# ScalarE's evacuations of PSUM banks take TensorE's order in the attention; GpSimd's sums in the recurrent mixer's gates go to VectorE

## The chip, the cores and the metric

The program runs on one core of a Trainium2 chip. A core has five engines that take their instructions in order, each from its own queue: TensorE (PE in the profile; its weight loads are PEld), VectorE (DVE), ScalarE (ACT), GpSimd (POOL) and SyncE (SP), which here only starts transfers. Matmul results land in PSUM, which this kernel divides into eight banks of 128 x 512 float32. The metric is the device time of one execution in microseconds (us).

## The reference, cut to what matters

Two layers run over 1024 positions of width 1024. Layer 0 mixes tokens with dilated window attention, layer 1 with a gated linear recurrence (HGRN2). Behind each mixer stand an output projection, a layer norm, a squared-ReLU MLP and another layer norm.

```python
for i in range(DEPTH):                      # DEPTH = 2
    if i % 2 == 0: y = dilated_attention_mixer(x, attn_w_in, attn_w_out)
    else:          y = hgrn2_mixer(x, hgrn_w_in, hgrn_w_out, hgrn_norm_g, lbs[i])
    x = layer_norm(ALPHA * x + y, ...)
    x = layer_norm(ALPHA * x + square(relu(x @ w_up)) @ w_down, ...)

# attention: 16 heads of 64, three groups (window, dilation) = (128,1), (512,4), (2048,16):
#   rotary q and k, a banded softmax, p @ v, then a mix of the three groups
#   by their softmax denominators

# hgrn2_mixer, 8 heads of 128, chunks of 64 positions:
log_f = logaddexp(log(lb), log1p(-lb) + log_sigmoid(z))    # z = forget projection
key   = (1 - lb) * sigmoid(-z)
b     = cumsum(log_f)                                      # inside a chunk
q_dec, k_dec = silu(q_raw) * exp(b), key * exp(-b)
kv    = einsum(key * exp(b_last - b), v)                   # one 128 x 128 matrix a chunk
state = exp(b_last) * state + kv                           # scan over 16 chunks
o     = causal(q_dec @ k_dec.T) @ v + q_dec @ state
```

## The kernel before, in words

All large products are float32 split into a high and a low part, so each product is three matmuls: high by high, high by low and low by high. The attention's input projection and both MLPs also use a seven-product scheme for 2 x 2 blocks.

**Attention.** `attention` walks 252 steps n: 12 groups of two units (a unit is a pair of heads in one dilation group), in each group the seven block products `ORDA = (2, 1, 6, 7, 4, 5, 3)`, in each of these three columns j. A step calls `product(n)`: 12 matmuls (lines 820 to 822) into a bank of the kind `mm` (there are three), and then the bank is read into SBUF. For i = 2, 6, 7, 4 ScalarE copies it (lines 843, 847, 849, 851, to tiles `e`, `vp`, `vT`), for i = 1, 5, 3 VectorE adds it. The next step of that column, where it goes on in the same bank, has to wait for this copy. Behind the product the step runs pieces of the group before: scores (`s`, two banks), transposes of the probabilities (`ppt`, line 636) or of v (`vpt`), copied by ScalarE to `pts` (line 639) or `vn` (line 546), the product with v (lines 665 and 667) into the one bank of the kind `o`, copied by ScalarE to `og` (lines 627, 673 and 676), and the transposes of the softmax statistics (`mpt`, lines 711 and 714), which use the bank `o` too and so wait until `og` was copied out. `vpt`, `ppt` and the broadcasts `fb` share the two banks `pt`. Last the step prepares weights five steps ahead: ScalarE rounds them to the high part (`H`, line 487), VectorE subtracts for the low part (line 495).

**What sets the order.** `in_order` ties TensorE's and VectorE's instructions of these steps to the order in which they are written. ScalarE is not tied (but for steps 30 to 33): a scheduler that estimates durations puts its instructions into a queue order before the program runs, and on the chip the queue is then strictly in order. `behind(i, names)` adds an order between instructions of one engine without a semaphore.

**Recurrent mixer.** `hgrn` runs 8 heads. For each head, three projections (forget, query, input) by two halves, then `gate`: for the forget projection a chain of ScalarE passes (absolute value, exponential, logarithm) and VectorE passes over 128 x 1024 (head 0: twice 128 x 512) that ends in `ls` (the log of the forget gate), a scan `a` (line 1854), the sum `z + a1` on GpSimd (line 1856), and two exponentials; for the query projection another chain with a sum on GpSimd (line 1870). The pieces of a head run during the projections of the next head: `kv(0)` and `kv(1)` (line 1771) fill banks with the chunks' matrices, VectorE runs the recurrence over them (line 1780, states 1 to 7 in `stA`, 8 to 15 in `stB`), and `omat(0)`, `omat(1)` (lines 1793 and 1798) multiply by the states. `omat(1)` writes into a bank `s` that the recurrence of `kv(1)` must have read first.

## Time and profile before

| what | value |
|---|---|
| median of 3 runs | 2743.94 us (2741.07 to 2744.34) |
| the profiled execution's own time | 2744.21 us |
| its span, first to last instruction | 2742.4 us |
| mean granted TensorE clock | 0.997 |
| busy: PE, DVE, ACT, POOL | 98%, 75%, 51%, 3% |
| PE busy in 0 to 900 us (attention) | 882.08 of 900 |
| PE busy in 900 to 1045 us (its tail, the output projection) | 138.16 of 145 |
| PE busy in 1045 to 1680 us (MLP) | 630.61 of 635 |
| PE busy in 1680 to 2040 us (recurrent mixer) | 356.58 of 360 |
| PE busy in 2040 to 2742 us (output projection, MLP) | 693.77 of 702 |

Busy time is a union of intervals; idle time of PE in a stretch is the stretch less the busy time. A row of a timeline gives start and length in us, engine, line, operation, tiles, shape and count; the bracket behind it gives the idle time before it and what ended that. In the list of waits the three numbers are the total, the count and the longest wait.

### The profile page before, as it was taken

The page shows a single profiled execution, that of the slowest core. Times are in us where ns is not written, and L with a number is a line of the kernel's source. Part 1 is how long each engine was busy: PE and PEld are TensorE (multiplying, and loading weights), DVE is VectorE, ACT ScalarE, POOL GpSimd, SP SyncE. Part 2 cuts the span into 40 slices and gives each one's busy share as a digit, 9 for nine tenths or more (in the row PEclk, how much of TensorE's full clock was granted, in tenths as well). Part 3 has the DMA queues.
Part 4 walks back from the last instruction along what each step waited for, and adds up shares of the span by engine and source line. Part 5 has one row for each costly group of instructions (what it writes and reads, how often), then busy time and mean ns, then how long its engine had stood idle before and what let it go on. Part 6 is the DMA issues. An engine that isn't in the chain of part 4 may idle for free.

```text
span 2742.4 us, 44173 instructions
## 1 busy us (share of the span) xinstructions
PE 2701.2 (98%) x16256; PEld 2200.8 (80%) x16256; DVE 2055.6 (75%) x3876; ACT 1385.1 (51%) x3043; POOL 68.8 (3%) x46
## 2 busy tenths in 40 slices
PE   9999999999999999999999999999999999999998
PEld 7787887787787777888888888788878888888887
DVE  8868877787787778776696687566578886678687
ACT  5554555455554556444554345555552544445443
POOL 0000000000000002000000000011100100000000
PEclk9999999999999999999999999999999999999999
DMA  8877666767767434554575752011232464485653
GB/s 300 273 223 230 210 219 198 234 204 234 227 214 257 115 109 156 192 194 150 204 268 165 239 169 93 32 47 47 74 127 100 157 221 163 150 299 181 220 179 127
DMA packets 208153, 493.67 MB, mean 180 GB/s; under 512 B 30016, under 2 KB 44864, under 8 KB 207936
## 3 DMA queue, kind: packets, MB, share of 16 engines
q1 hardware_dynamic: 206688, 489.53, 53.1%
q8 instruction: 128, 2.10, 0.3%
q10 hardware_dynamic: 1248, 1.31, 0.2%
q14 instruction: 89, 0.73, 0.1%
HBM read 362.69 MB, written 94.11 MB: 167 GB/s over the span
## 4 chain that ended last, share of the span: by engine, by line
PE 87%; DVE 7%; ACT 2%; DMA 2%; issue 1%; SPq 0%; POOL 0%; DVEq 0%; ACTq 0%; POOLq 0%
PE pmm L822 7%; PE pmm L820 7%; PE pmm L821 7%; PE pup L1342 7%; PE pup L1340 7%; PE pup L1341 7%; PE pdy L1491 4%; PE pdy L1495 4%; PE pdy L1494 4%; PE pdx L1494 3%; PE pdx L1495 3%; PE pdx L1491 3%; PE pmm L192 3%; PE pmm L193 3%; PE pmm L194 3%; PE pmm L206 2%
## 5 line engine op out<-in xcount | busy, mean ns | idle before, releaser
L820 PE MATMUL pmm<-xh,H 128*128 128x512 f32 x1008 | 404.5, 401 | 1.5 <-ACT H L487 1.5
L822 PE MATMUL pmm<-xh,H 128*128 128x512 f32 x1008 | 396.2, 393 | 3.2 <-DVE H L495 2.9
L821 PE MATMUL pmm<-xl,H 128*128 128x512 f32 x1008 | 394.4, 391 | 0.8 <-DVE xl L158 0.7
L822 PEld LDWEIGHTS pmm<-xh,H 128*128 128x128 f32 x1008 | 189.8, 188 | 48.4 <-DVE H L495 7.7
L820 PEld LDWEIGHTS pmm<-xh,H 128*128 128x128 f32 x1008 | 190.5, 189 | 39.9 <-ACT H L487 2.6
L821 PEld LDWEIGHTS pmm<-xl,H 128*128 128x128 f32 x1008 | 190.5, 189 | 38.3 <-DVE xl L158 1.6
L1491 PE MATMUL pdy<-dT,dS 128*128 128x512 f32 x512 | 199.2, 389 | 0.0
L1494 PE MATMUL pdy<-dT,dS 128*128 128x512 f32 x512 | 199.2, 389 | 0.0
L1495 PE MATMUL pdy<-dT,dS 128*128 128x512 f32 x512 | 199.2, 389 | 0.0
L157 ACT ACTIVATE dS<-dr 128x512 fp32r<-128x512 f32 x192 | 119.3, 622 | 67.4 <-PE pdy L1495 36.4
L192 PE MATMUL pmm<-f0nh,wh 128*128 128x512 f32 x384 | 153.3, 399 | 0.0
L193 PE MATMUL pmm<-f0nl,wh 128*128 128x512 f32 x384 | 149.9, 390 | 0.0
L194 PE MATMUL pmm<-f0nh,wl 128*128 128x512 f32 x384 | 149.8, 390 | 0.0
L158 DVE TENSOR_TENSOR dS<-dr,dS 128x512 fp32r<-128x512 f32 x192 | 131.3, 684 | 8.9 <-ACT dS L157 8.9
L583 ACT ACTIVATE p<-p,stats 128x192 f32<-128x192 f32 (+1 forms) x256 | 108.7, 428 | 53.8 <-DVE stats L580 53.5
L157 ACT ACTIVATE dT<-hold 128x512 fp32r<-128x512 f32 x128 | 80.1, 626 | 80.6 <-DVE hold L1470 33.2
L1301 ACT ACTIVATE H<-wc 128x512 fp32r<-128x512 f32 x128 | 77.2, 625 | 78.5 <-DVE wc L1294 47.8
L1494 PEld LDWEIGHTS pdy<-dT,dS 128*128 128x128 f32 x512 | 96.1, 188 | 20.0
L1495 PEld LDWEIGHTS pdy<-dT,dS 128*128 128x128 f32 x512 | 96.1, 188 | 20.0
L1491 PEld LDWEIGHTS pdy<-dT,dS 128*128 128x128 f32 x512 | 96.1, 188 | 19.8
L580 DVE CUSTOM_DVE_ANT_0 p<-s,mask 128x192 f32<-128x192 f32 (+1 forms) x256 | 70.7, 332 | 45.0 <-PE s L567 32.3
L487 ACT ACTIVATE H<-wc 128x512 fp32r<-128x512 f32 x108 | 66.5, 629 | 70.1 <-DVE wc L479 67.5
(430 smaller groups left out, 6924.8 us busy)
## 6 DMA issues: line engine op xcount, KB each, us to landing
xh<-xtd SPq DMA_DIRECT2D x110, 512.0 KB
xl<-xtd SPq DMA_DIRECT2D x110, 512.0 KB
dr<-hd SPq DMA_DIRECT2D x192, 256.0 KB
dr<-in_w_down_dram SPq DMA_DIRECT2D x128, 256.0 KB
rot<-e SPq DMA_DIRECT2D x192, 128.0 KB
wa<-in_w_up_dram SPq DMA_DIRECT2D x48, 512.0 KB
wb<-in_w_attn_dram SPq DMA_DIRECT2D x36, 512.0 KB
wa<-in_w_attn_dram SPq DMA_DIRECT2D x33, 512.0 KB
```

Of the source, the lines that this page charges most:

```text
L157: act(hi, raw, AF.Copy)
L192: nc.tensor.matmul(o, wh[:, k], xs.h(k), start=k == 0, stop=False)
L193: nc.tensor.matmul(o, wh[:, k], xs.l(k), start=False, stop=False)
L194: nc.tensor.matmul(o, wl[:, k], xs.h(k), start=False, stop=k == NK - 1)
L820: nc.tensor.matmul(o, wh, hi[k // 2][:, c], start=begin and k == 0, stop=False, skip_group_check=True)
L821: nc.tensor.matmul(o, wh, lo[k // 2][:, c], start=False, stop=False, skip_group_check=True)
L822: nc.tensor.matmul(o, wl, hi[k // 2][:, c], start=False, stop=end and k == 3, skip_group_check=True)
L1340: nc.tensor.matmul(o, wh, xf.h(b, k), start=begin and k == 0, stop=False, skip_group_check=True)
L1341: nc.tensor.matmul(o, wh, xf.l(b, k), start=False, stop=False, skip_group_check=True)
L1491: nc.tensor.matmul(o[q], h, T_[:, L], start=begin, stop=False, skip_group_check=True)
L1494: nc.tensor.matmul(o[q], h, T_[:, R], start=False, stop=False, skip_group_check=True)
L1495: nc.tensor.matmul(o[q], l, T_[:, L], start=False, stop=end, skip_group_check=True)
```

## The change

**In the attention** a helper `evict` replaces `act` at every ScalarE copy out of a PSUM bank: the products' copies, `vn`, `pts`, `og`, `ml` and `sr`. It notes the instruction, and when the loop over the steps is done, each noted instruction is put `behind` the one noted before it. So these copies keep the order in which they are written, which is the order in which TensorE fills the banks. The other ScalarE instructions (`H`, the exponentials) are as free as before. The copies of the last group's pieces, which run after the loop, are not tied.

**In the gates** the constants change: `low` is exp(-max(C, -43)), C keeps only what lies below -43, `nA` is -A, `CA` is gone. The first logarithm takes `low` as scale and bias, so that it yields log(1 + E) less the bound's term C in one pass; with that the pass of VectorE on line 1852 (add C, then maximum with A) and the one on line 1853 (add) become one. Both sums of GpSimd are now VectorE's.

```diff
     def attention(pre, hc):
+        out_of = []
+        def evict(*args, **kw):
+            act(*args, **kw)
+            out_of.append(latest())
...
-                    act(vn[:, j * 512:(j + 1) * 512], pt, AF.Copy)
+                    evict(vn[:, j * 512:(j + 1) * 512], pt, AF.Copy)
...
         order.__exit__()
+        for i, j in zip(out_of, out_of[1:]):
+            behind(j, [i.name])
+        out_of.clear()
...
-        CA = c8("CA")
-        v.tensor_sub(CA, C, A)
+        low = c8("low")
+        v.tensor_scalar(low, C, -43.0, None, op0=ALU.max)
+        v.tensor_sub(C, C, low)
+        act(low, low, AF.Exp, scale=-1.0)
+        nA = c8("nA")
+        v.tensor_scalar(nA, A, -1.0, None, op0=ALU.mult)
...
                 act(a1, z, AF.Abs)
                 act(a1, a1, AF.Exp, scale=-1.0)
-                act(a1, a1, AF.Ln, bias=one)
+                act(a1, a1, AF.Ln, scale=low[:, hd:hd + 1], bias=low[:, hd:hd + 1])
                 nc.vector.scalar_tensor_tensor(ls, z, 0.0, a1, op0=ALU.min, op1=ALU.subtract)
                 nc.vector.scalar_tensor_tensor(z, z, 0.0, a1, op0=ALU.max, op1=ALU.add)
-                act(a1, ls, AF.Abs, bias=CA[:, hd:hd + 1])
+                act(a1, ls, AF.Abs, bias=nA[:, hd:hd + 1])
                 act(a1, a1, AF.Exp, scale=-1.0)
                 act(a1, a1, AF.Ln, bias=one)
-                nc.vector.tensor_scalar(ls, ls, C[:, hd:hd + 1], A[:, hd:hd + 1], op0=ALU.add, op1=ALU.max)
-                nc.vector.tensor_add(ls, ls, a1)
+                nc.vector.scalar_tensor_tensor(ls, ls, A[:, hd:hd + 1], a1, op0=ALU.max, op1=ALU.add)
                 nc.vector.tensor_tensor_scan(a1, sm[:, c], ls, 0.0, op0=ALU.mult, op1=ALU.add)
-                nc.gpsimd.tensor_add(z, z, a1)
+                nc.vector.tensor_add(z, z, a1)
...
-                nc.gpsimd.tensor_add(a3, a3, cur["a"][:, c])
+                nc.vector.tensor_add(a3, a3, cur["a"][:, c])
```

The diff moves instructions, and three places show how. A row gives the line, the operation, the tiles written and read, the shape and a count.

The first place is ScalarE's queue in the attention, in the third group, around the statistics `sr` that the profile has at 265.8 us. Of the kernel before:

```order
L849 ACTIVATE e<-pmm 128x512
L639 ACTIVATE pts<-ppt 128x384 x2
L487 ACTIVATE H<-wb 128x512
L849 ACTIVATE vp<-pmm 128x512
L851 ACTIVATE e<-pmm 128x512
L849 ACTIVATE e<-pmm 128x512
L676 ACTIVATE og<-o 128x2x256
L487 ACTIVATE H<-wc 128x512
L716 ACTIVATE sr<-mpt 32x128
```

And of the changed kernel, where L361 is the line in `evict` and L493 is the rounding of `H`:

```order
L361 ACTIVATE e<-pmm 128x512
L493 ACTIVATE H<-wb 128x512
L361 ACTIVATE e<-pmm 128x512
L361 ACTIVATE og<-o 128x2x256
L361 ACTIVATE pts<-ppt 128x384 x2
L493 ACTIVATE H<-wc 128x512
L361 ACTIVATE vp<-pmm 128x512
L493 ACTIVATE H<-wc 128x512 x2
L361 ACTIVATE e<-pmm 128x512
L361 ACTIVATE sr<-mpt 32x128
```

The second copy of `e` and the copy of `og` stood behind `pts`, `vp` and a copy of the next block product; now they stand ahead of all three. The order of TensorE's and VectorE's instructions in the attention is the same as before.

The second place is VectorE's queue in the recurrent mixer, in the second head (the profile has it from 1728 us), with the recurrence of the first head in between. Before:

```order
L1780 SCALAR_TENSOR_TENSOR stA<-stA,dec,kvps 128x128 x3
L1853 TENSOR_TENSOR ls<-ls,a_17045 128x1024
L1780 SCALAR_TENSOR_TENSOR stA<-stA,dec,kvps 128x128
L1854 SCALAR_TENSOR_TENSOR a_17045<-smask,ls 128x1024
L1780 SCALAR_TENSOR_TENSOR stA<-stA,dec,kvps 128x128 x2
L1780 SCALAR_TENSOR_TENSOR stB<-stA,dec,kvps 128x128
```

Now (L1793 is the recurrence, L1865 the joined pass, L1866 the scan, L1868 the sum that was GpSimd's):

```order
L1793 SCALAR_TENSOR_TENSOR stA<-stA,dec,kvps 128x128 x3
L1865 SCALAR_TENSOR_TENSOR ls<-ls,hc_A,a_17047 128x1024
L1793 SCALAR_TENSOR_TENSOR stA<-stA,dec,kvps 128x128
L1866 SCALAR_TENSOR_TENSOR a_17047<-smask,ls 128x1024
L1793 SCALAR_TENSOR_TENSOR stA<-stA,dec,kvps 128x128
L1868 TENSOR_TENSOR ze<-ze,a_17047 128x1024
L1793 SCALAR_TENSOR_TENSOR stA<-stA,dec,kvps 128x128
L1793 SCALAR_TENSOR_TENSOR stB<-stA,dec,kvps 128x128
```

State 7, the last one in `stA`, now comes behind the sum over 128 x 1024.

The third place is TensorE's queue at the same moment, the end of `omat(0)` of the first head. Before:

```order
L1793 MATMUL ho<-vn,aT 64x128 x2
L1798 MATMUL ho<-stA,qe 64x128 x2
L1771 MATMUL kvps<-vn,k2n 64x128 x14
L192 MATMUL pmm<-f0nh,wh 128x512
```

Now:

```order
L1806 MATMUL ho<-vn,aT 64x128 x2
L1811 MATMUL ho<-stA,qe 64x128
L1784 MATMUL kvps<-vn,k2n 64x128 x3
L1811 MATMUL ho<-stA,qe 64x128
L1784 MATMUL kvps<-vn,k2n 64x128 x11
L192 MATMUL pmm<-f0nh,wh 128x512
```

Three of the next matrices' matmuls moved ahead of the one that reads state 7. It is the only change in TensorE's order.

## The prediction

> **What bounds the kernel now.** I read the page's first part, then the list of TensorE's waits, then the timelines around the longest of them. The page:

> ```profile
> span 2742.4 us, 44173 instructions
> PE 2701.2 (98%) x16256; PEld 2200.8 (80%) x16256; DVE 2055.6 (75%) x3876; ACT 1385.1 (51%) x3043; POOL 68.8 (3%) x46
> ```

> TensorE is busy for 2701.2 of 2742.4 us. The change removes none of its matmuls, so it can win only out of the 41.2 us in which TensorE idles, and out of time in which its clock is low. The waits of TensorE (releaser; total, count, longest):

> ```profile
> PE mpt L714 <- ACT og L676: 6.4, 3, 2.1
> PE mpt L711 <- ACT og L673: 3.0, 3, 1.0
> PE pmm L822 <- DVE H L495: 2.9, 5, 1.2
> ...
> PE ho L1798 <- DVE stB L1780: 1.6, 1, 1.6
> ...
> PE ho L1793 <- DVE stB L1780: 1.4, 1, 1.4
> ```

> The two longest entries are one pattern: the transposes of the statistics need the bank `o`, which ScalarE has not copied out yet. The last two belong to the recurrent mixer. All other entries are start-up, weights or the layers' ends, which the change does not touch.

> **Attention: the six waits for `og`.** The first long one:

> ```profile
> 254.50 0.39 PE L822 MATMUL pmm<-xh,H 128*128 128x512 f32 x1
> 256.33 0.22 PE L667 MATMUL o<-pts,vn 64*64 64x64 f32 x1
> 260.14 0.60 ACT L849 ACTIVATE vp<-pmm 128x512 f32<-128x512 f32 x1 [1.68 <-PE pmm L822]
> 263.34 0.60 ACT L851 ACTIVATE e<-pmm 128x512 f32<-128x512 f32 x1 [2.60 <-PE pmm L822]
> 263.84 0.59 ACT L849 ACTIVATE e<-pmm 128x512 f32<-128x512 f32 x1
> 264.31 1.08 ACT L676 ACTIVATE og<-o 128x512 f32<-128x512 f32 x1
> 265.45 0.33 PE L714 MATMUL mpt<-ident,stats 128*128 128x128 f32 x1 [2.14 <-ACT og L676]
> ```

> The product for the second `e` ends by 254.9, the bank `o` is full at 256.55. ScalarE could copy both then, but its queue has `vp` and the next product's `e` (L851) ahead, and these wait for TensorE (1.68 and 2.60 us of idleness). So `og` starts 7.8 us after its data and TensorE stands for 2.14 us. In the changed queue both stand ahead of `pts` and `vp`. ScalarE then does `e` (0.59), `og` (1.08) and two `pts` from about 256.6 and is done by 259.2; `vp` is ready at 260.1, and TensorE comes to `mpt` at 263.3. The wait is gone with 4 us to spare. The 1.0 us kind is the same, one dilation group on:

> ```profile
> 414.18 0.19 ACT L583 ACTIVATION_READ_ACCUMULATOR p<-p,stats 128x1 f32 x1
> ...
> 417.56 0.60 ACT L851 ACTIVATE e<-pmm 128x512 f32<-128x512 f32 x1 [2.13 <-PE pmm L822]
> ...
> 418.52 0.61 ACT L673 ACTIVATE og<-o 128x512 f32<-128x512 f32 x1
> ```

> Here four exponentials now come ahead of `e`, `og` and `pts`. At this place of the profile the last of them ends at 414.4, so `og` (0.61) behind one `e` (0.60) is out by about 415.6, against about 418.1 where TensorE wants the bank (1.0 us before `og` ends). Two `pts` get late by some 3 us, to about 416.5; the next transposes, which need their banks, start here:

> ```profile
> 417.36 0.82 PE L636 MATMUL ppt<-ident,p 128*128 128x128 f32 x6
> ```

> That leaves about 0.9 us, the thinnest cover of the change; without it the 1.0 us would be back. I take off 6.4 + 3.0 = **9.4 us**. The order among the copies costs nothing by itself: none is put behind one that TensorE fills later, so no copy waits longer than its own data needs. SP's queue now has one weight load behind the four small loads of `ml` and one copy of `vT`:

> ```profile
> 271.78 0.54 SPq L460 DMA_DIRECT2D wa<-in_w_attn_dram  x1
> ...
> 283.84 1.67 ACT L487 ACTIVATE H<-wa 128x512 fp32r<-128x512 f32 x3
> ```

> It is issued 12 us ahead of its rounding, so a shift by five such issues costs 0.

> **The clock behind these waits.** A table of stretches (length, PE, PEld, DVE, ACT, POOL, granted clock, DMA share, GB/s) and one matmul:

> ```profile
> 263.00:273.00 10.00, 7.86 (x70) 6.17 (x72) 4.93 (x7) 5.01 (x9) 0.00 (x0) 1.00 0.98 358
> 494.00:504.00 10.00, 8.35 (x44) 6.62 (x46) 4.13 (x7) 4.56 (x9) 0.00 (x0) 0.83 0.85 324
> 726.00:736.00 10.00, 8.01 (x36) 6.28 (x38) 4.48 (x7) 4.90 (x9) 0.00 (x0) 0.83 0.90 337
> 1046.00:1054.00 8.00, 5.76 (x17) 3.94 (x17) 6.35 (x12) 2.06 (x5) 0.52 (x1) 0.79 0.50 183
> ...
> 498.52 0.63 PE L820 MATMUL pmm<-xh,H 128*128 128x512 f32 x1
> ```

> Behind two of the three waits of 2.1 us the clock falls, and a matmul takes 0.63 instead of 0.39 us. The loss is 10 x (1 - 0.83) = 1.7 us each time. Where the wait is gone I expect the dip gone: 2 x 1.7 = **3.4 us**. The dip at 1046 follows other waits (8 x 0.21 = 1.7 us); it stays in my sum, and may go or stay with the changed phase.

> [...]

> **Gates: VectorE and GpSimd.** The second head, in order of time:

> ```profile
> 1732.17 2.28 DVE L1854 TENSOR_TENSOR_SCAN a<-smask,ls 128x1024 f32<-128x1024 f32 x1
> 1734.38 0.70 DVE L1780 SCALAR_TENSOR_TENSOR stA<-stA,dec,kvps 128x128 f32<-128x128 f32 x2
> 1741.95 1.22 DVE L1869 SCALAR_TENSOR_TENSOR a<-qe,a 128x1024 f32<-128x1024 f32 x1
> 1743.24 2.35 POOL L1870 TENSOR_TENSOR a<-a,a 128x1024 f32<-128x1024 f32 x1 [6.29 <-DVE rms L1808]
> 1743.41 2.20 DVE L1809 TENSOR_SCALAR rms<-rms 128x4 f32<-128x4 f32 x1
> 1745.53 1.21 DVE L158 TENSOR_TENSOR wl<-wr,wh 128x1024 fp32r<-128x1024 f32 x1
> 1746.74 0.34 DVE L1780 SCALAR_TENSOR_TENSOR stB<-stB,dec,kvps 128x128 f32<-128x128 f32 x1
> ...
> 1743.64 0.44 PE L1793 MATMUL ho<-vn,aT 128*64 128x128 f32 x4 [1.39 <-DVE stB L1780]
> 1747.13 0.43 PE L1798 MATMUL ho<-stB,qe 128*64 128x128 f32 x2 [1.55 <-DVE stB L1780]
> ```

> A VectorE operation on 128 x 4 takes 2.20 us, because it lies under GpSimd's sum (2.35 us) and ends with it; the rounding (1.21) comes next, and only then the last state. TensorE waits 1.39 + 1.55 = 2.94 us. The bare sums on VectorE take what a like pass takes, 1.22 us. Per head VectorE loses the 2.2 us under GpSimd once or twice and the pass of line 1852, and gains two passes:

> ```profile
> L1856 POOL TENSOR_TENSOR ze<-ze,a 128x1024 f32<-128x1024 f32 (+1 forms) x9 | 19.3, 2148 | 296.3 <-ACT a L1866 108.6 <-DVE a L1854 85.7 <-DVE rms L1808 67.6
> L1852 DVE TENSOR_SCALAR ls<-ls,hc_C,hc_A 128x1024 f32<-128x1024 f32 x7 | 5.7, 808 | 1.3 <-ACT a L1849 1.3
> ```

> That is -0.81 + 2 x 1.22 = +1.63 us of work against up to 4.4 us unblocked. In the changed queue states 14 and 15 stand ahead of the pass of line 1869, so from about 1741.7 nothing of `omat(1)` waits: **-2.94 us**.

> But a new wait appears at state 7. The scan ends at 1734.45; state 6 takes 0.26, the moved sum 1.14, state 7 0.26: 1736.1. TensorE without it:

> ```profile
> 1734.75 0.82 PE L1798 MATMUL ho<-stA,qe 128*64 128x128 f32 x4 [0.19 <-DVE stA L1780]
> 1735.49 1.09 PE L1771 MATMUL kvps<-vn,k2n 64*64 64x128 f32 x28
> ```

> It would begin state 7's matmul at 1735.1, and the three matmuls moved ahead fill 0.2 us. I take **+0.8 us** (bounds 0, if the queue slips as it did before, and 1.1).

> In the later heads TensorE does not wait before, though only just:

> ```profile
> 1783.37 0.34 DVE L1780 SCALAR_TENSOR_TENSOR stB<-stB,dec,kvps 128x128 f32<-128x128 f32 x1
> 1783.65 0.44 PE L1793 MATMUL ho<-vn,aT 128*64 128x128 f32 x4
> ```

> There the states now all stand ahead of the joined pass, which is about 1.6 us earlier, and the moved sums come behind them: 0. The logarithm keeps its shape, with a scale read per partition. No row has that form; I price it at 0 and bound it by one more pass of line 1852 (0.81 us), 9 times, off the path since TensorE waits for no such pass. The constants add two operations on 128 x 8 on VectorE and one on ScalarE, once: 0, bounded by 3 x 0.34 = 1.0 us from the nearest row above.

> **Sum.** 9.4 + 3.4 + 2.94 - 0.8 = 14.9 us. The profiled execution took 2744.21 (1.8 around the span); less 14.9 is 2729.3. The median is 0.3 below that execution, so the forecast is **2729.0**.

> **Rivals.**
> 1. *The dips stay* : if a dip needs more than the gap, the waits go but 3.4 us of low clock come back elsewhere, 2732.4. For it: the stretch at 263 has a gap of 2.1 us and clock 1.00, so the gap alone doesn't make a dip. Against it: two of the three gaps have a dip directly behind them. Chance 0.10.
> 2. *The wait moves to `pt`*: in the groups with the 1.0 us wait, `pts` behind four exponentials holds the two `pt` banks, and `ppt` stands instead of `mpt`; a state or two in the gates also late. Then 3.0 and 2.1 us are not won: 2734.1, or 2737 if the later `pts` cost another microsecond in each. For it: only 0.9 us of cover. Chance 0.14.
> 3. *ScalarE's estimate is as wrong as before elsewhere*: roundings `H` now stand ahead of copies, a late one holds the whole chain, and waits of 1 to 2 us return in most of the 12 groups: 12 x 1 takes back 12: 2741, no change. For it: `H` reads loads and VectorE's rotated weights, which may be late. Against it: by the first fence TensorE's longest wait for `H` is 1.2 us, and all five are 2.9 us together. Chance 0.06.
> 4. *Slower: VectorE's two sums land on the path in every head.* Price 7 x 2 x 1.22 + 2 x 2 x 0.69 = 19.8 us, and the 2.94 us stay: 2744.0 + 19.8 - 12.8 = 2751. It decides where the sums of line 1856 or 1870 come ahead of a state that TensorE already wants, as in the second head. Against it: there the order is unique to that head. Chance 0.03.

> That the copies don't follow TensorE is ruled out by the queues shown.

> **Numbers.** The forecast has 0.67; with rivals 1 and 2 nearly all of the chance is faster. By about 0.2% (5.5 us) a change can be told from none, so faster means under 2738.5: 0.67 + 0.10 + 0.12 = 0.89; same 0.08; slower 0.03. Low end: the forecast less the other dip (1.7), the new wait (0.8) and 2.5 for where the windows of the clock fall (the runs lie 3.3 us apart): 2724. High end: rival 2's upper case, and a dip: 2738.

> **What would show it.** Right: no `mpt` wait for `og` in TensorE's list, clock 1.00 in the three stretches 12 us or less earlier, no `stB` wait, one `stA` wait of about 0.8 us near 1724. Wrong: `ppt` waiting for `pts`, `H` waits above 3 us, granted clock under 0.9 in new stretches, or `ho` waiting in later heads.

## The result

The changed kernel takes **2728.25 us** (median of 4 runs, 2726.57 to 2729.02) against 2743.15 us of the kernel before (2741.07 to 2744.34, 4 runs): a ratio of 0.9946, 95% interval 0.9928 to 0.9963, so 14.9 us less. Forecast were 2729.0 us. Measured again on another chip, it was 2727.26 against 2744.03 us (16.8 less), ratio 0.9942 (0.9928 to 0.9956). The profiled execution has a span of 2727.2 us, 15.2 less than before.

The page of the changed kernel and its list of TensorE's waits (releaser; total, count, longest):

```profile
span 2727.2 us, 44137 instructions
PE 2698.6 (99%) x16256; PEld 2199.0 (81%) x16256; DVE 2043.0 (75%) x3887; ACT 1387.0 (51%) x3044; POOL 28.3 (1%) x28
...
PE pmm L828 <- DVE H L501: 2.9, 5, 1.2
...
PE pup L1351 <- DVE H L1318: 1.3, 1, 1.3
...
PE ho L1811 <- DVE stA L1793: 1.0, 2, 0.6
```

The idle time fell from 41.2 to 28.6 us. No wait of `mpt` for `og` is left, none of `ho` for `stB`; for `stA` there are two small ones, where before has one of 0.2 us. This is the first of the six places in the changed kernel, as a timeline (L361 is the copy in `evict`, L720 the transposes `mpt`), and the place with the thinnest cover:

```profile
254.92 0.58 ACT L361 ACTIVATE e<-pmm 128x512 f32<-128x512 f32 x1
258.50 1.08 ACT L361 ACTIVATE og<-o 128x512 f32<-128x512 f32 x1 [3.01 <-PE pmm L827]
263.43 0.27 PE L720 MATMUL mpt<-ident,stats 128*128 128x128 f32 x1
...
412.02 0.58 ACT L361 ACTIVATE og<-o 128x512 f32<-128x512 f32 x1
412.50 0.86 ACT L361 ACTIVATE pts<-ppt 128x384 f32<-128x384 f32 x2
415.38 0.82 PE L642 MATMUL ppt<-ident,p 128*128 128x128 f32 x6
```

`og` is out by 259.6, and `mpt` runs at 263.4 without a wait: 3.8 us to spare. At the thin place `pts` is done by 413.4 and `ppt` starts at 415.4: 2.0 us to spare. Three stretches of 10 us, from the places of the former long waits on (length, PE, PEld, DVE, ACT, POOL, granted clock, DMA share, GB/s) have no idle time and the full clock:

```profile
263.00:273.00 10.00, 10.00 (x96) 8.14 (x95) 6.28 (x16) 5.06 (x11) 0.00 (x0) 1.00 0.98 374
490.50:500.50 10.00, 10.00 (x95) 8.17 (x94) 6.22 (x16) 5.47 (x13) 0.00 (x0) 1.00 0.93 368
718.30:728.30 10.00, 10.00 (x96) 8.17 (x95) 6.20 (x16) 5.48 (x13) 0.00 (x0) 1.00 0.97 375
```

From the first `mpt` to the last, before took 863.4 us and the changed kernel 851.0: 12.4 of the 15.2 us. For the recurrent mixer, the stretch from its first transposes (`hpt`) to its last (`opt`), of before and then of the changed kernel, in the same columns:

```profile
1717.00:2061.31 344.31, 340.89 (x2529) 277.73 (x2527) 218.76 (x360) 185.79 (x277) 33.48 (x14) 1.00 0.19 65
```

```profile
1705.42:2046.74 341.32, 340.36 (x2529) 277.51 (x2527) 207.61 (x367) 186.25 (x277) 0.00 (x0) 1.00 0.20 66
```

That is 3.0 us less, of which 2.5 are idle time of TensorE (3.42 to 0.96). The rest of the program adds up to about zero: the start is 0.3 us later, and a wait of 0.7 us for a weight is new at 1168 us. At the start of the first MLP the clock stays low for two windows in place of one (below), but TensorE's wait for the first low part is shorter (1.3 for 1.8 us), and the stretch from the last `mpt` to that layer's last `lnpt` (the transposes of the layer norm) takes 110.2 us, and 110.4 before.

In the second head VectorE and TensorE now stand so:

```profile
1723.19 1.21 DVE L1868 TENSOR_TENSOR ze<-ze,a 128x1024 f32<-128x1024 f32 x1
1724.32 0.34 DVE L1793 SCALAR_TENSOR_TENSOR stA<-stA,dec,kvps 128x128 f32<-128x128 f32 x1
...
1727.61 0.16 DVE L1817 TENSOR_SCALAR rms<-rms 128x4 f32<-128x4 f32 x1
...
1723.32 0.43 PE L1811 MATMUL ho<-stA,qe 128*64 128x128 f32 x2 [0.37 <-DVE stA L1793]
1724.71 0.43 PE L1811 MATMUL ho<-stA,qe 128*64 128x128 f32 x2 [0.59 <-DVE stA L1793]
```

The sum (1.21 us) stands ahead of state 7, and the matmul that reads state 7 waits 0.59 us for it. The wait of 0.37 us ahead of it is for state 6, which comes right behind the scan and ahead of the sum; before it was 0.19 us. So 0.77 us were added, where 0.8 was forecast. The elementwise operations on 128 x 4 take 0.14 to 0.17 us each.

### The profile page after: what moved, and what is told of

It reads as the page before. It is cut to its first block, busy times and chain, and to the rows that moved or that the text cites. A ratio compares the mean times of both kernels' runs of the same rounds, so it can differ in the third digit from the quotient of the medians.

```text
span 2727.2 us, 44137 instructions
## 1 busy us (share of the span) xinstructions
PE 2698.6 (99%) x16256; PEld 2199.0 (81%) x16256; DVE 2043.0 (75%) x3887; ACT 1387.0 (51%) x3044; POOL 28.3 (1%) x28
## 4 chain that ended last, share of the span: by engine, by line
PE 90%; DVE 6%; ACT 1%; DMA 1%; issue 1%; SPq 0%; DVEq 0%; ACTq 0%
PE pup L1351 7%; PE pup L1349 7%; PE pmm L828 7%; PE pup L1350 7%; PE pmm L826 7%; PE pmm L827 7%; PE pdy L1504 4%; PE pdy L1503 4%; PE pdy L1500 4%; PE pmm L192 3%; PE pdx L1503 3%; PE pdx L1504 3%; PE pdx L1500 3%; PE pmm L194 3%; PE pmm L193 3%; PE pmm L204 2%
## 5 line engine op out<-in xcount | busy, mean ns | idle before, releaser
L158 DVE TENSOR_TENSOR dS<-dr,dS 128x512 fp32r<-128x512 f32 x192 | 130.9, 682 | 9.3 <-ACT dS L157 9.3
L493 ACT ACTIVATE H<-wc 128x512 fp32r<-128x512 f32 x108 | 66.6, 629 | 75.3 <-DVE wc L485 73.3
```

## The experiments

Times are medians; "before" is the kernel before, measured beside each version on the same chip. Its medians, on four chips, are 2744.0 to 2745.0 us.

### The two parts apart

The attention's part alone: the gates and their constants of before, with the chain.

```diff
-                nc.vector.tensor_add(z, z, a1)
+                nc.gpsimd.tensor_add(z, z, a1)
...
-                act(a1, a1, AF.Ln, scale=low[:, hd:hd + 1], bias=low[:, hd:hd + 1])
+                act(a1, a1, AF.Ln, bias=one)
```

> The attention's part of the change alone: ScalarE's copies are chained, the gates are those of before. My theory: the two parts are independent. The six waits for og (9.4 us) and the two clock dips behind them (3.4 us) go, and the two waits for stB (1.4 + 1.6 us) stay, so the time is 12 to 13 us under before: about 2730.8 us (2729.5 to 2732.5). Rival (the dips only move): the waits go, the low clock returns elsewhere, about 2734. Rival (the gates' part matters for the attention too, by its constants or a shifted phase): not between these, at the changed kernel's 2728 or above 2734.

Measured: 2727.90 us (2727.04 to 2729.07), before 2744.99; ratio 0.9938 (0.9924 to 0.9951). TensorE's waits for the states are those of before:

```profile
PE ho L1807 <- DVE stB L1789: 1.6, 1, 1.6
PE ho L1802 <- DVE stB L1789: 1.4, 1, 1.4
```

So the waits are as my theory had them, but the time is not: 17.1 us less, where 12 to 13 were expected. Its profiled execution has a span 15.4 us shorter than before's: from the first `mpt` to the last it takes 849.4 us, 14.0 less, and it has no dip of the clock near 1050 us, where before has one (108.8 for 110.4 us from the last `mpt` to the last `lnpt`); it has one at 38 us instead.

The gates' part alone: the changed kernel without the chain.

```diff
-        for i, j in zip(out_of, out_of[1:]):
-            behind(j, [i.name])
```

> The gates' part alone: the sums on VectorE and the joined logarithm, without the chain of copies. My theory: the six waits for og and the dips behind them stay as before, the two waits for stB (2.94 us) go, and two waits for stA of about 1.0 us together come: 2 us under before, about 2741 (2739.5 to 2742.5). Rival (VectorE's two added sums cost on the path in every head): above 2743.2. Rival (the changed kernel's gain is mostly from the gates): under 2735.

Measured: 2742.44 us, before 2744.99; ratio 0.9990 (0.9982 to 0.9999). As expected, 2.5 us, and the waits for `og` are there to the tenth:

```profile
PE mpt L720 <- ACT og L361: 6.4, 3, 2.1
PE mpt L717 <- ACT og L361: 3.0, 3, 1.0
```

In this profile all three long waits are followed by a dip of the clock, where before had two, and there is one more at 39 us.

Because 17.1 and 2.5 us do not add up to the changed kernel's gain, both were run side by side.

> The changed kernel once more, beside the attention's part alone and on the same chip, because on two chips the two had the same time, although the traces give the gates' part 2.7 us between the first transposes of the recurrent mixer and its last. My theory: the two parts add up, and what hid it are dips of the clock at other places (at start-up, at the first layer's MLP), which come or not by the phase of the clock's windows of 3.41 us: so this one is 1.5 to 3.5 us under the attention's part alone. Rival (the gates' gain is given back later in the program): within 1 us of each other.

> The attention's part alone once more, beside the changed kernel. My theory: 1.5 to 3.5 us over the changed kernel in the same call; the recurrent mixer's stretch from its first transposes to its last takes 344.0 us against 341.3. Rival: within 1 us.

Measured: changed 2727.26 us (2726.31 to 2728.65), attention alone 2728.11 (2727.30 to 2729.92), before 2744.03. The difference is 0.85 us: by the medians my expectation (1.5 to 3.5) failed and the rival's number holds. By the traces the stretch of the recurrent mixer is 344.00 us for the attention alone and 341.30 for the changed kernel, as expected, and no later stretch is longer by more than 0.2 us. So the gain isn't given back behind the mixer. The two profiled executions lie 1.7 us apart (2726.41 and 2728.11). Against the attention alone, the changed kernel has 2.7 us less in the mixer, 0.5 less ahead of the first `mpt`, 0.3 more in the attention and 1.1 more between the attention and the mixer. There it has a dip of the clock at 1036 us (110.4 us from the last `mpt` to the last `lnpt`, the other 108.8); the other has its one dip at 26 us. So in these two profiles the place of a dip hides part of the 2.7 us.

Whether the gates' part brings the dip near 1036 us more often is left open: of the nine profiles that have a part of the gates and no wait for `og`, seven have it; of the two of the attention alone, none has; but before, without the gates' part, has it too. The mean granted clock of the five runs (0.9980 against 0.9986) doesn't settle it: the clock also falls for the last microseconds of a profile (from 2719 us on in the one, from 2723 in the other), when TensorE has no work left.

### The place of `og`

The first of two smaller ties: each `og` ahead of the next seven copies, the other copies free.

```diff
-        for i, j in zip(out_of, out_of[1:]):
-            behind(j, [i.name])
+        for k, i in enumerate(out_of):
+            if i.name in is_og:
+                for j in out_of[k + 1:k + 8]:
+                    behind(j, [i.name])
```

> The changed kernel with a smaller tie: each copy og stands ahead of the next seven copies, and the other copies are as free as before. My theory is that only og behind copies of later products made the six waits: no wait of mpt for og, time as the changed kernel, 2727 to 2730. Rival (the order among pts, e and sr matters by itself): waits of 1 to 2 us come back on ppt or mpt, 2731 to 2735. Rival (og was not the cause): as before in the attention, 2741.

Measured: 2727.21 us (2726.48 to 2728.19), before 2744.99, ratio 0.9935 (0.9922 to 0.9949). No `mpt` waits for `og`. So the place of `og` alone makes the six waits; the order among the other copies is not needed to end them.

The second: all copies chained but `og`.

```diff
-                    evict(og[:, hb * 512:(hb + 1) * 512], o, AF.Copy)
+                    act(og[:, hb * 512:(hb + 1) * 512], o, AF.Copy)
```

> The changed kernel with every copy chained but og. In this queue og still stands ahead of the copies of the later products at the places of the six waits, since those now stand behind pts. My theory (only the place of og in the queue counts, not the tie itself): no wait of mpt for og, 2727 to 2730. Rival (the tie on og is needed): the waits of 2.1 and 1.0 us return, 2736 to 2741.

Measured: 2728.42 us (one run), no wait of `mpt`. The tie on `og` itself is not needed: with `vp` and the next product's `e` put behind `pts`, the scheduler places `og` early by itself. The first place in this kernel:

```profile
255.94 0.58 ACT L361 ACTIVATE e<-pmm 128x512 f32<-128x512 f32 x1
259.51 1.08 ACT L682 ACTIVATE og<-o 128x512 f32<-128x512 f32 x1 [2.99 <-PE pmm L827]
264.44 0.27 PE L720 MATMUL mpt<-ident,stats 128*128 128x128 f32 x1
```

Both ties work, and in both no copy of a later product stands ahead of `og`.

### The sums and the logarithm

Both keep the chain. The sums on VectorE with the two passes of before (and the logarithm and the constants of before):

```diff
-                nc.vector.scalar_tensor_tensor(ls, ls, A[:, hd:hd + 1], a1, op0=ALU.max, op1=ALU.add)
+                nc.vector.tensor_scalar(ls, ls, C[:, hd:hd + 1], A[:, hd:hd + 1], op0=ALU.add, op1=ALU.max)
+                nc.vector.tensor_add(ls, ls, a1)
```

> The chain of copies, with the sums on VectorE and the two logarithm passes of before. My theory: what removes the two waits for stB is that GpSimd's sum no longer holds VectorE's small operation (2.20 us); the joined logarithm does nothing on the path. So the waits for stB go, the waits for stA of about 1.0 us come, and the time is the changed kernel's within 1 us: 2727.5 to 2729.5. Rival (the joined pass is needed, since two sums more fill VectorE): waits for stB or for states in the later heads, 2730 or above.

The joined logarithm with the sums on GpSimd:

```diff
-                nc.vector.tensor_add(z, z, a1)
+                nc.gpsimd.tensor_add(z, z, a1)
...
-                nc.vector.tensor_add(a3, a3, cur["a"][:, c])
+                nc.gpsimd.tensor_add(a3, a3, cur["a"][:, c])
```

> The chain of copies, with the joined logarithm and the sums still on GpSimd. My theory: VectorE's operation on 128x4 still takes some 2.2 us under GpSimd's sum and the two waits for stB stay (2.9 us): 2730 to 2732, as with the chain alone. Rival (the pass saved is what frees VectorE): the waits for stB go too, 2728.

Measured: sums 2725.97 us (2724.78 to 2726.37, ratio 0.9932, 0.9915 to 0.9948), logarithm 2730.31 (2729.15 to 2731.67, ratio 0.9948, 0.9934 to 0.9963), before 2744.27. The logarithm alone, VectorE, GpSimd and TensorE in the second head:

```profile
1730.09 2.21 DVE L1822 TENSOR_SCALAR rms<-rms 128x4 f32<-128x4 f32 x1
1732.21 1.21 DVE L158 TENSOR_TENSOR wl<-wr,wh 128x1024 fp32r<-128x1024 f32 x1
1733.41 0.34 DVE L1793 SCALAR_TENSOR_TENSOR stB<-stB,dec,kvps 128x128 f32<-128x128 f32 x1
1729.92 2.35 POOL L1882 TENSOR_TENSOR a<-a,a 128x1024 f32<-128x1024 f32 x1 [6.29 <-DVE rms L1821]
1730.32 0.44 PE L1806 MATMUL ho<-vn,aT 128*64 128x128 f32 x4 [1.36 <-DVE stB L1793]
1733.81 0.43 PE L1811 MATMUL ho<-stB,qe 128*64 128x128 f32 x2 [1.55 <-DVE stB L1793]
```

The operation on 128 x 4 again takes 2.21 us and ends with GpSimd's sum; the rounding and the state follow. With the sums on VectorE, and the logarithm as before:

```profile
1726.61 0.35 DVE L1789 SCALAR_TENSOR_TENSOR stB<-stB,dec,kvps 128x128 f32<-128x128 f32 x1
1726.88 0.16 DVE L1818 TENSOR_SCALAR rms<-rms 128x4 f32<-128x4 f32 x1
...
PE ho L1807 <- DVE stA L1789: 0.8, 2, 0.6
```

0.16 us, and no wait for `stB`. (The time with the sums lies 1.5 us under the expected range.) The stretch of the recurrent mixer is 341.36 us with the sums (341.32 with both), and 344.02 with the logarithm (344.05 without it). The sums are the whole gain of this part; the joined logarithm is worth nothing on the path. GpSimd's sum (2.35 us) and VectorE's operation on 128 x 4 (2.21 us) end together, at 1732.27 and 1732.30 us, and without the sum beside it the operation takes 0.16 us. By what the one holds up the other, no run here shows.

### State 7

The sum behind state 7 (and the query's pass behind the last state), in the changed kernel:

```diff
+                        if hd == 0 and c == 6:
+                            behind(sum1[0], [latest().name])
...
+                if hd == 1:
+                    behind(latest(), [sum1[1].name])
```

> The changed kernel, but in the second head the sum over 128x1024 stands behind state 7 of the first head, and the pass ahead of the query's sum behind the last state. My theory: the two waits for stA (0.37 + 0.59 us) shrink to 0.2 us or less and no wait for stB comes, so the span is 0.8 us shorter: 2727.5, which only the list of waits can tell. Rival (VectorE is short of time here, so a state put ahead makes another late): the waits for stA go, waits for stB or for the weights' low part of 0.5 us or more come, 2728 or above.

Measured: 2727.18 us (2725.86 to 2728.24), before 2744.99, ratio 0.9934 (0.9922 to 0.9947). One wait of 0.4 us for `stA` is left, more than the 0.2 expected, and none for `stB`:

```profile
PE ho L1816 <- DVE stA L1794: 0.4, 1, 0.4
...
1705.63:2046.18 340.55, 340.18 (x2528) 277.49 (x2527) 207.52 (x367) 186.32 (x277) 0.00 (x0) 1.00 0.20 66
```

The wait that is left is the one for state 6, behind the scan, which the edit does not move. The stretch is 0.77 us shorter, as expected; the times cannot tell it.

The states first, the sums on VectorE, the logarithm of before:

> The chain of copies and the sums on VectorE, the two logarithm passes of before, and the states put first in the second head as in the experiment with state 7. My theory: the joined logarithm is worth nothing on the path, so the recurrent mixer's stretch takes 340.5 us as with the joined logarithm and the states first; the whole is 17 to 19 us under before (ratio 0.9930 to 0.9938), the fastest of the versions or level with the fastest. Rival (the pass that the joined logarithm saves is needed once the states stand first, since the logarithm's chain ends 1.2 us later in every head): the stretch is 341 us or more, with waits for stA or stB of 0.5 us or more.

Measured: 2727.16 us (2724.62 to 2728.96), before 2744.40, ratio 0.9934 (0.9921 to 0.9948). The stretch is 340.33 us, so the joined logarithm is not needed here either. By its list of waits one of 0.2 us for `stA` is left. In its profile (2728.19 us) the clock stays low for three windows from 1032 us, and the stretch from the last `mpt` to the last `lnpt` takes 111.7 us, 1.3 more than with one window; another execution of the same kernel took 2724.62.

### What makes the clock fall

The dips were the disputed term of the sum. Here the changed kernel gets gaps of many lengths: GpSimd copies an operand of 27 products onto itself, so TensorE waits.

```diff
+            left = GAPS[n // 3 % len(GAPS)] if n % 21 in (4, 10, 16) and 42 <= n < 231 else 0
+            while left:
+                part_ = hi[0][:, :min(left, 1024)]
+                nc.gpsimd.tensor_copy(part_, part_)
+                left -= min(left, 1024)
```

> The changed kernel with gaps put into TensorE's work: at 27 places of the attention GpSimd copies columns of an operand onto themselves (1536 to 6144 columns in ten steps), so that the next product has to wait. No rows price such a copy, so the gaps may be from 0 to 10 us; the trace gives each. Theory A (the clock is judged in fixed windows of 3.4 us and falls for the next window where TensorE idled over half of one, which the dips of before suggest: 1.9, 2.0 and 2.1 us of idleness in the window ahead, and 1.6 us without a dip): no dip behind a gap under 1.7 us, one behind every gap over 3.4 us, and behind those between in a share of about gap / 3.4; the starts of the dips lie a whole number of 3.4 us apart. Theory B (a gap of 3.4 us or more is needed): no dip behind gaps under 3.4 us. Theory C (the dips come from what TensorE does, not from gaps): no more dips than the one or two of the changed kernel. Time: the changed kernel's plus the sum of the gaps, plus 1.7 us for each dip.

Measured: 2885.9 us (one run). The gaps came out between under 0.8 and 9.5 us. The clock's edges that fall into a run of matmuls lie on a grid: in this trace 191.16, 655.37 and 757.76 us, which are 136 and 30 times 3.413 us apart; with the gates' part alone 267.27, 499.38 and 731.49, twice 68 times. Cut into windows on that grid, three traces show whole windows at clock 1.00 or 0.50 and none between: 843 here, 802 of before, 802 of the gates alone. Some windows of the gaps' kernel (columns as above):

```profile
399.37:402.79 3.41, 1.22 (x5) 1.03 (x6) 1.24 (x2) 2.00 (x4) 2.08 (x2) 1.00 0.49 158
402.79:406.20 3.41, 3.41 (x12) 2.17 (x15) 0.05 (x1) 0.00 (x0) 0.00 (x0) 0.50 0.51 90
...
648.55:651.96 3.41, 1.48 (x7) 0.93 (x6) 3.34 (x5) 1.25 (x3) 2.94 (x3) 1.00 0.89 215
651.96:655.37 3.41, 3.41 (x9) 2.64 (x9) 3.41 (x6) 0.52 (x1) 0.00 (x0) 0.50 0.90 247
931.85:935.27 3.41, 1.56 (x7) 0.94 (x5) 3.35 (x5) 1.64 (x3) 3.04 (x3) 1.00 0.90 230
935.27:938.68 3.41, 2.90 (x12) 2.17 (x12) 3.41 (x5) 0.53 (x1) 0.46 (x1) 1.00 0.98 256
```

A gap of 1.94 us that lay in one window (busy 1.48, idle 1.93) brought a dip; one of 2.36 us of which 1.85 lay in one window did not. Over the three traces, 31 windows at full clock were followed by one at half: their idle times go from 1.91 to 3.41 us. Of the others none had more than 1.85. Behind a window that was itself at half clock the bound is lower: 16 with 0.60 us of idleness or more were followed by another, 30 with 0.52 or less by the full clock. So theory A holds, with the bound a little above half a window in these three; B (3.4 us of idleness) and C fall. The bound is not sharp, though. The other eleven traces, cut in the same way, have 22 more windows at full clock that were followed by one at half: 18 with 1.89 us of idleness or more, and four with only 1.64 to 1.73 us. Two of the four are these, near the start of the program, with matmuls of full width:

```profile
35.53:38.95 3.42, 1.78 (x7) 1.24 (x8) 3.29 (x5) 1.36 (x4) 0.00 (x0) 1.00 1.00 406
38.95:42.36 3.41, 3.41 (x10) 2.65 (x9) 3.39 (x5) 1.58 (x3) 0.00 (x0) 0.50 0.50 198
...
23.08:26.49 3.41, 1.70 (x7) 0.80 (x6) 3.38 (x6) 1.52 (x2) 0.00 (x0) 1.00 0.97 396
26.49:29.91 3.42, 3.42 (x10) 2.64 (x9) 3.38 (x6) 0.63 (x1) 0.00 (x0) 0.51 0.34 140
```

(The first two rows are of the states first with the sums, the others of the attention alone, measured again.) What decides between 1.6 and 1.9 us of idleness is open.

The costs fit roughly. The gaps over 0.8 us that the copies made add up to 108 us. TensorE was busy for 96 us at half clock, and for 6 us in the changed kernel's profile, so 90 / 2 = 45 us more are lost: together 153, measured 2885.9 - 2728.3 = 157.6.

The same in before, around the dip at 497 us:

```profile
493.72:497.13 3.41, 1.48 (x7) 1.27 (x8) 1.83 (x3) 3.00 (x6) 0.00 (x0) 1.00 1.01 384
497.13:500.54 3.41, 3.41 (x9) 2.68 (x9) 0.07 (x1) 1.22 (x4) 0.00 (x0) 0.50 0.89 353
500.54:503.96 3.41, 3.41 (x28) 2.62 (x29) 2.51 (x4) 0.61 (x2) 0.00 (x0) 1.00 0.64 234
```

At the first wait, at 263 us, the window of before with the most idleness had 1.71 us of it and no dip came. The same wait lies in one window with 2.02 us where the gates' part ran alone, and there it has one.

### The first MLP's start

The changed kernel's dip near 1036 us lasts for two windows:

```profile
1030.11:1033.52 3.41, 1.68 (x12) 1.18 (x12) 3.41 (x9) 2.99 (x7) 0.31 (x1) 1.00 1.00 386
1033.52:1036.94 3.42, 2.62 (x7) 1.12 (x5) 3.35 (x6) 1.77 (x5) 0.96 (x1) 0.50 1.03 381
1036.94:1040.35 3.41, 2.94 (x7) 2.37 (x8) 3.30 (x7) 0.00 (x0) 0.00 (x0) 0.50 0.10 36
```

The first of them has 1.73 us of idleness, less than any window that brought a dip in the gaps' kernel. It holds transposes of 128 columns (`lnpt`); whether those count for less than matmuls is open, and a window of the attention alone with such transposes and 1.53 us of idleness, at 1028 us, brought no dip. The second holds the first part of the wait for the low part of `H` (0.79 us idle), and so the low clock stays. To take this wait away, VectorE's low part was put ahead of a statistics pass of the last layer norm (with the states first, as above):

```diff
+                if last_ln:
+                    first_low.append(latest().name)
+                    behind(last_ln.pop(0), first_low)
+                    last_ln.clear()
...
```

> The changed kernel with the states first (as in the experiment with state 7), and at the start of the first layer's MLP VectorE's first low part of H put between the two statistics passes of the last layer norm, 2.7 us ahead of its place. My theory: TensorE's wait of 1.3 to 2.0 us for that low part goes, the window of 3.41 us then holds 1.7 us of idleness at most and no dip follows (1.7 us, in the changed kernel's profile 3.4 us): 3 to 5 us under the changed kernel, 2723 to 2726. Rival (the layer norm that is put later holds VectorE's queue, which waits for ScalarE's part of it): new waits of 2 us or more in the MLP's first 30 us, no gain or a loss, 2728 or above.

Measured: 2727.76 us (2724.14 to 2728.33), before 2744.03, ratio 0.9939 (0.9927 to 0.9952): no gain over the changed kernel beside it (2727.26), so my expectation failed, and the rival's time (2728 or above) nearly came. Two of the five executions were faster than any of the changed kernel's beside it (2724.14 and 2725.61, against 2726.31). The wait and the dip did go in the profile: the stretch from the last `mpt` to the last `lnpt` takes 109.2 us, and 110.2 to 110.5 in the profiles with a dip there of one or two windows. But VectorE now waits 2.6 us at a later low part, and new waits of 1.5 and 1.9 us come:

```profile
1039.86 0.69 DVE L1323 TENSOR_TENSOR H<-wa,H 128x512 fp32r<-128x512 f32 x1 [2.64 <-ACT H L1315]
...
PE lnpt L254 <- DVE fs L331: 1.9, 1, 1.9
...
PE pup L1360 <- DVE H L1323: 1.7, 2, 1.5
```

These waits take back a part: from the last `mpt` to the first `hpt` the profile is 0.5 us shorter than the changed kernel's beside it, and 0.8 us shorter in the mixer. What hides this are 2.9 us more at the start and in the attention, which this edit doesn't touch.

No version beats the changed kernel clearly. The sums alone have the lowest ratio (0.9932), but its interval overlaps all the others with the chain, and the chips differ.

## Why the prediction was right

- **The six waits (9.4 us)**: right, in place and size. All are gone, and the tie on `og` alone does the same (2727.21 us), so the cause was the one named. The cover was larger than reckoned where it was thinnest: 2.0 us, not 0.9, because the exponentials there ended 2.7 us earlier than reckoned (411.6 for 414.4) and the transposes behind only 2.0 us earlier. The bank was copied out later than reckoned at the first place (259.6, not 258.2, since by the trace `og` was released by a matmul of the next product), which the 4 us of cover took.
- **The dips (3.4 us)**: right for the profile that the sum was made against (clock 1.00 in all three stretches), and the reading that gaps of 2.1 us can suffice was right: in the kernel with gaps one of 1.94 us did. But the term was one draw. Whether a gap of 2.1 us brings a dip depends on where the windows' grid falls in that execution: of the three long waits two had a dip in before's profile, and all three with the gates alone (at the first, 1.71 us of idleness lay in one window of before, and 2.02 us with the gates alone). The attention's part alone took 17.1 us off where the sum has 12.8 for it; part of that is the dip near 1050 us, which its profile doesn't have. A larger share of dips in before's runs would explain more, and their mean clock (0.995 to 0.997, the attention's 0.998 to 0.999) points that way; no trace of those runs shows it. The 2.5 us that the low end takes off for where the clock's windows fall are shown by no run; the traces show windows of 3.413 us, and the changed kernel's four runs lie 2.45 us apart (2726.57 to 2729.02).
- **The dip at 1046, "stays in my sum"**: it stayed, for two windows instead of one in the profile, but the stretch around it is no longer than before (110.2 for 110.4 us). That was a draw as well: four of the eleven profiles without the six waits don't have it.
- **The waits for `stB` (2.94 us)**: right, and shown to come from GpSimd's sums: without these they go, with the joined logarithm alone they stay.
- **The new wait at state 7 (0.8 us)**: it came with 0.59 us, and the wait for state 6 just ahead, which the prediction left as it was, grew from 0.19 to 0.37; together 0.77 us more. Putting the states first takes 0.77 us off the stretch.
- **The later heads and the logarithm (0)**: right. Over 128 x 1024 the logarithm with scale and bias from tiles takes 1247 ns, the second logarithm, with a bias alone, 1147 ns; the 0.1 us a pass is off the path, as the stretches of the mixer with and without the joined logarithm show (341.32 and 341.36 us).
- **The stretch as a whole**: 3.0 us shorter, where the terms say 2.1. The waits give 2.2 of it, the rest is idle time of under 0.2 us a piece that the sum left out, and 0.5 us of busy time. The total hides this: the changed kernel is only 0.85 us under the attention's part alone.

Of the rivals, "the dips stay" had the right objection (the phase matters) and the wrong outcome here; the wait did not move to `pt` and no `H` held the chain; no sum landed on the path but the one at state 7, and VectorE's work fell by 12.6 us on the page. That the total was met within 1 us is partly luck. By the profiles the attention gave 12.4 us where 12.8 were reckoned, the mixer 3.0 where 2.1, and the rest took 0.2 back; and measured again the same change gave 16.8 us.

## What to carry to other kernels

Where one in-order engine copies out banks for several consumers, look for a ready copy that stands behind one whose data come later: here moving that one copy was enough, and the tie of everything was not needed. A wait's price on TensorE is its length plus a chance of a window at half clock: in this case up to 1.7 us (half a window) for a gap of which 1.91 us or more lie in one window of 3.41 us, and behind four windows with 1.64 to 1.73 us too. Take such a term as a draw, not as a constant. A term under 3 us is read from a stretch of the trace between two fixed instructions, since the dips move the total by as much.

## What the hardware showed that was not expected

The three long waits stand about 232 us apart (232.0 and 232.5 us where the gates' part ran alone), which is 68 windows, so their dips should tend to come or stay away together. The times of the kernels with these waits spread over 6.8 us (15 runs of before) and 7.0 us (11 runs of the gates alone), those of the kernels without them over 2.0 to 4.3 us (5 runs each). The spreads are measured, but they don't show it: a spread grows with the number of runs, and the standard deviations are 1.9 and 2.0 us with the waits and 0.9 to 2.0 us without. That the dips come together is argued, not shown.
